# Matmul with batch norm: x and w loads on the SP and ACT queues, x casts on GpSimd, output copies on ScalarE

## The chip, the core and the metric

The kernel runs on one core of a Trainium2 chip. A core has five engines, each working through its own list of instructions in order: PE (TensorE, matmuls and transposes), DVE (VectorE), ACT (ScalarE), POOL (GpSimd) and SP (SyncE, which here only issues DMAs). Instructions on different engines wait for each other by semaphores; an instruction that waits holds up everything behind it on its engine. DMAs are issued from an engine's list and then run on 16 DMA engines that all queues share. The metric is the time of one execution in microseconds (us).

## The reference

```python
# x [16, 512, 1024], weight [1024, 768], gamma, beta [768], all f32
y = np.matmul(x, weight)                              # 8192 rows x 768 columns
mean = np.mean(y, axis=(0, 1), keepdims=True)         # one mean and variance per column
var = np.var(y, axis=(0, 1), keepdims=True)
y_norm = (y - mean) / np.sqrt(var + eps)
return (gamma * y_norm + beta).astype(np.float32)
```

No column can be normalized before its statistics over all 8192 rows are there.

## The kernel before

**Layout.** The 8192 rows of x are read in 32 loads of 256 rows (`load_x(q)`, L128, 1 MB each), two of which make one of 16 chunks of 512 rows (index c). The 768 columns are six tiles of 128 (index nt). The matmuls give y transposed, 128 columns by 512 rows, and one `mm(nt, c)` (L153) of eight matmuls is called a unit here. There are 96.

**A load.** A load is four DMAs, one for each quarter of k: quarter i goes into partitions 32i to 32i+31 of the tile `x_st`. Quarters 0 and 1 are issued by SP, 2 and 3 by POOL. The tile comes from the pool `stage`, which has three buffers; w loads (six, of 128 columns) and the output tiles `o_sb` use the same three. `cast_x(q, part)` (L133, ACT) turns half a load into bf16, `turn_x` (L147, DVE) turns it into `xT` by 32x32 blocks. `cast_w` (L120) is on DVE.

**A unit.** `mm` writes a PSUM tile `y_ps` (five buffers), `bn` (L159, DVE) takes its statistics, then `keep` (L164, ACT) copies it to SBUF as bf16 and frees it. In the program `keep` waits for `bn`.

**Two phases.** While x arrives, the first five chunks go through all six column tiles and the other eleven through tiles 0 to 2 (group A, 63 units in all). Then `finish` (L169 to L174) makes scale and shift for group A. Its output runs in 16 blocks of 512 rows beside the eleven units left of tile 3; then tile 3's output (eight blocks of 1024 rows) runs beside the units of tile 4, tile 4's beside those of tile 5, and tile 5's last. An output block is `norm` (L177, DVE), `turn_y` (L190, PE transposes into `o_ps`), `out_copy` (L198 on ACT or L200 on DVE, by turns) and `store` (L204, SP).

**Order.** Every step is put into a list of events with a due time worked out by hand (`at`, and the constants `W_US`, `Q_US`, `MM_US`). The list is sorted, and `seq` holds each engine to that order. So the numbers in the plan decide who stands behind whom in an engine's list, whatever the true durations are. `load_affine` (L103, L104) is one event with 12 small DMAs of gamma and beta on POOL, due when the last load has been planned.

Of the kernel before, what the change touches and what calls it, by code (L numbers as in the profile page):

```python
# [10 lines left out]
def kernel(  # L11
# [18 lines left out]
    nc = tc.nc  # L30
    f32 = mybir.dt.float32
# [8 lines left out]
    P = 128  # L40
    NT = N // P
    KQ = K // 4
    KT = K // P
# [4 lines left out]
    QU = QT // 2  # L48
    UP = 2
    QPC = CH // QR  # L50
    EARLY = 5
    STAGE = 3
    GA = 3
# [5 lines left out]
    stage = ctx.enter_context(tc.tile_pool(name="stage", bufs=STAGE))  # L59
    xbpool = ctx.enter_context(tc.tile_pool(name="xbpool", bufs=2))  # L60
    xtpool = ctx.enter_context(tc.tile_pool(name="xtpool", bufs=C - EARLY))
    ypool = ctx.enter_context(tc.tile_pool(name="ypool", bufs=(GA * C + (NT - GA) * EARLY) + 6))
    ypsum = ctx.enter_context(tc.tile_pool(name="ypsum", bufs=5, space=bass.MemoryType.PSUM))
# [21 lines left out]
    w_sb = singles.tile([P, KT, N], bf16)  # L85
# [10 lines left out]
    seq(nc.scalar.activation(warm, eps_sb, AF.Sqrt))  # L96


    xs, xb, xT, py, y, ops, ost, wst = {}, {}, {}, {}, {}, {}, {}, {}

    def load_affine():
# [3 lines left out]

    def load_w(part):

        n0 = part * P
        w_st = stage.tile([P, KT, P], f32, tag="st")
        wst[part] = w_st  # L110
        for i in range(4):
            eng = nc.sync if i < 2 else nc.gpsimd
            seq(eng.dma_start(  # L113
                w_st[32 * i:32 * i + 32],
                weight[KQ * i:KQ * (i + 1), n0:n0 + P].rearrange("(jj c) n -> c jj n", c=32),
            ))

    def cast_w(part):
        n0 = part * P
        seq(nc.vector.tensor_copy(w_sb[:, :, n0:n0 + P], wst.pop(part)))  # L120

    def load_x(q):
        x_st = stage.tile([P, QT, KQ], f32, tag="st")
        xs[q] = x_st
        rows = x_flat[q * QR:(q + 1) * QR].rearrange("(t r) k -> r t k", r=32)
        for i in range(4):
            eng = nc.sync if i < 2 else nc.gpsimd
            seq(eng.dma_start(x_st[32 * i:32 * i + 32], rows[:, :, KQ * i:KQ * (i + 1)]))  # L128

    def cast_x(q, part):  # L130
        x_bf = xbpool.tile([P, UP, KQ, 2], bf16, tag="xb")
        xb[q, part] = x_bf
        seq(nc.scalar.copy(  # L133
            x_bf.rearrange("p u k h -> p h u k"),
            xs[q].rearrange("p (h u) k -> p h u k", h=2)[:, :, part * UP:(part + 1) * UP, :],
        ))

    def turn_x(q, part):
        c, half = divmod(q, QPC)
        if half == 0 and part == 0:  # L140
            xT_sb = xtpool.tile([P, KT, CH], bf16, tag="xT")
            xT[c] = xT_sb
        src = xb.pop((q, part)).rearrange("p u k h -> p (u k h)").bitcast(f32)
        src = src.rearrange("p (u jj c) -> p u jj c", u=UP, c=32)
        dst = xT[c].rearrange("p jj m -> p (jj m)").bitcast(f32)
        dst = dst.rearrange("p (jj q u r) -> p q u jj r", jj=KT, q=QPC, r=32)
        seq(nc.vector.transpose(dst[:, half, part * UP:(part + 1) * UP], src))  # L147
# [64 lines left out]
    def at(t, fn, *args):  # L212
        events.append((t, len(events), fn, args))

    W_US, Q_US, MM_US = 1.0, 2.7, 1.75
    t = 0.0
    arrive = {}
    order = [("w", 0), ("w", 1), ("w", 2), ("x", 0), ("x", 1), ("w", 3), ("w", 4), ("w", 5)]
    order += [("x", q) for q in range(2, C * QPC)]
    freed = []  # L220
    for j, (kind, n) in enumerate(order):
        issue = t - 3.0
        if j >= STAGE:
            issue = max(issue, freed[j - STAGE] + 0.01)
        if kind == "w":
            at(issue, load_w, n)
            t += W_US
            at(t + 2.2, cast_w, n)
            freed.append(t + 2.2)
        else:  # L230
            at(issue, load_x, n)
            t += Q_US
            for part in range(QU // UP):
                at(t + 2.5 + 1.1 * part, cast_x, n, part)
                at(t + 3.7 + 1.1 * part, turn_x, n, part)
                freed.append(t + 2.5 + 1.1 * part) if part == QU // UP - 1 else None
            arrive[n] = t + 6.0

    at(t, load_affine)
    pe = 0.0  # L240
# [1 line left out]
    def unit(nt, c, span):  # L242
        nonlocal pe
        pe = max(pe, arrive[c * QPC + QPC - 1])
        at(pe, mm, nt, c)
        at(pe + 1.9, bn, nt, c)
        at(pe + 2.7, keep, nt, c)
        pe += span

    count = [0]  # L250

    def outputs(nts, t0, step, tiles, parts):

        rows = tiles * parts * P
        for b in range(M // rows):
            m0 = b * rows
            tb = t0 + step * b
            for c in range(m0 // CH, (m0 + rows) // CH):
                for nt in nts:
                    at(tb - 1.2, norm, nt, c)  # L260
            key = (nts[0], b)
            for part in range(parts):
                ti = tb + step / parts * part
                at(ti, turn_y, (key, part), nts, m0 + part * tiles * P, tiles)
                eng = "act" if count[0] % 2 == 0 else "dve"
                count[0] += 1
                at(ti + 0.9, out_copy, key, part, parts, eng)
            at(tb + step + 1.2, store, key, nts, m0, tiles * parts)

    for c in range(C):  # L270
        for nt in range(NT if c < EARLY else GA):
            unit(nt, c, MM_US)
    ga = list(range(GA))
    at(pe + 1.9, finish, ga)
    outputs(ga, pe + 6.0, 2.24, 2, 2)
    for nt in range(GA, NT):
        for c in range(EARLY, C):
# [42 lines left out]
```

## Time and profile before

| | |
|---|---|
| median of 3 runs | 311.28 us (309.02 to 312.35) |
| the profiled execution | 311.01 us |
| its span (first to last instruction) | 309.2 us |
| mean granted TensorE clock | 0.932 |
| PE busy, share of the span | 211.1 us, 68% |
| DVE busy | 172.5 us, 56% |
| ACT busy | 157.2 us, 51% |
| POOL busy | 51.6 us, 17% |
| HBM read, written | 36.71 MB, 25.17 MB |

The profiled execution lies 1.81 us above its own span (start and end), and 0.27 us below the median. Rows of a timeline give start, duration, engine, source line, operation, out<-in, shapes, count, and in brackets the idle time before with what ended it. Rows of the waits give who waited for whom, the sum in us, how often, and the longest. Rows of the groups give line, engine, operation, shapes and count, then busy us, mean ns of one, and idle us before with its releaser.

### The profile page before, as it was taken

What the parts mean: (1) busy time and instruction counts of PE and PEld (TensorE: products, weight loads), DVE (VectorE), ACT (ScalarE), POOL (GpSimd) and SP (SyncE); (2) the same over time, 40 slices, a digit from 0 to 9 for tenths busy, and PEclk for the clock granted to TensorE, in tenths of its full rate; (3) what the DMA queues carried; (4) which work ended last, traced back from release to release, by engine and by line L of the source; (5) the groups of instructions that cost most, each with busy time, mean ns of one, the idle gap of its engine ahead of it and who ended that gap; (6) DMA issues with size and microseconds to landing.
All of it is one profiled execution on the core that took longest, in us unless ns stands there. A gap on an engine that the chain in (4) does not pass through costs nothing.

```text
span 309.2 us, 3408 instructions
## 1 busy us (share of the span) xinstructions
PE 211.1 (68%) x1132; PEld 102.6 (33%) x1152; DVE 172.5 (56%) x312; ACT 157.2 (51%) x194; POOL 51.6 (17%) x95
## 2 busy tenths in 40 slices
PE   0006984667465658566855899998988999996630
PEld 0002432223222223222322344455544544543620
DVE  0131454535545455354454653689999866876851
ACT  1050667566766767657676753254553443434320
POOL 5414321212122122231225400000000000000000
PEclk9999999959999797998799999999999999998575
DMA  7999999999999999999999000029997884665698
GB/s 179 213 218 209 224 211 231 210 217 218 214 230 215 219 223 214 218 210 221 223 219 215 11 0 2 0 93 342 334 339 270 293 235 136 170 199 167 192 274 225
DMA packets 60177, 62.10 MB, mean 201 GB/s; under 512 B 3456, under 2 KB 55680, under 8 KB 60160
## 3 DMA queue, kind: packets, MB, share of 16 engines
q1 hardware_dynamic: 54080, 43.52, 57.2%
q0 software_dynamic: 6080, 18.36, 27.3%
q8 instruction: 9, 0.15, 0.2%
q14 instruction: 8, 0.07, 0.1%
HBM read 36.71 MB, written 25.17 MB: 200 GB/s over the span
## 4 chain that ended last, share of the span: by engine, by line
DMA 45%; PE 25%; ACT 11%; DVE 11%; issue 4%; POOL 1%; SPq 1%; ACTq 0%; DVEq 0%; POOLq 0%
DMA x_st<-in_x_dram 37%; PE y_ps L153 19%; ACT x_bf L133 9%; PE o_ps L190 6%; DMA w_st<-in_weight_dram 4%; DVE y_sb L177 4%; DVE o_sb L200 3%; DMA out_dram<-o_sb 3%; DVE stats L159 2%; ACT y_sb L164 1%; ACT o_sb L198 1%; SPq L128 1%; DVE mv L169 1%; POOL w_st L113 1%; DMA gamma_sb<-in_gamma_dram 1%
## 5 line engine op out<-in xcount | busy, mean ns | idle before, releaser
L153 PE MATMUL y_ps<-xT_sb,w_sb 128*128 128x512 bf16 x748 | 184.1, 397 | 73.9 <-ACT y_sb L164 45.7
L153 PEld LDWEIGHTS <-w_sb 128*128 128x128 bf16 x768 | 76.6, 101 | 169.8 <-issue 87.5
L133 ACT CAST x_bf<-x_st 128x1024 bf16<-128x1024 f32 x64 | 83.5, 1329 | 69.4 <-DMA x_st<-in_x_dram 66.1
L147 DVE STREAM_TRANSPOSE xT_sb<-x_bf 128x512 f32<-128x512 f32 x64 | 45.3, 709 | 79.5 <-ACT x_bf L133 79.5
L164 ACT CAST y_sb<-y_ps 128x512 bf16<-128x512 f32 x96 | 55.7, 580 | 49.6 <-DVE stats L159 49.6
L159 DVE BATCH_NORM_STATS2 stats<-y_ps 128x6 f32<-128x512 f32 x96 | 64.5, 676 | 15.5 <-PE y_ps L153 15.5
L128 POOL DMA_DIRECT2D x_st<-in_x_dram x64 | 37.1, 585 | 111.1 <-ACT x_bf L133 96.1
L190 PE MATMUL o_ps<-ident,y_sb 128*128 128x128 bf16 x384 | 34.5, 237 | 14.5 <-DVE y_sb L177 13.1
L200 DVE CAST o_sb<-o_ps 128x768 f32<-128x768 bf16 (+1 forms) x28 | 29.8, 1065 | 14.1 <-PE o_ps L190 5.9
L190 PEld LDWEIGHTS <-y_sb 128*128 128x128 bf16 x384 | 27.1, 106 | 26.8 <-DVE y_sb L177 21.0
L198 ACT CAST o_sb<-o_ps 128x768 f32<-128x768 bf16 (+1 forms) x28 | 25.0, 891 | 20.8 <-PE o_ps L190 11.9
L177 DVE TENSOR_SCALAR y_sb<-y_sb,scale,shift 128x512 bf16<-128x512 bf16 x96 | 33.6, 402 | 0.0
L120 DVE CAST w_sb<-w_st 128x1024 bf16<-128x1024 f32 x6 | 4.2, 694 | 20.6 <-DMA w_st<-in_weight_dram 20.6
L113 POOL DMA_DIRECT2D w_st<-in_weight_dram x12 | 7.3, 612 | 6.1 <-ACT x_bf L133 5.6
L103 POOL DMA_DIRECT2D gamma_sb<-in_gamma_dram x6 | 3.3, 551 | 3.4 <-DMA x_st<-in_x_dram 3.3
L104 POOL DMA_DIRECT2D beta_sb<-in_beta_dram x6 | 3.3, 547 | 1.9 <-DMA x_st<-in_x_dram 1.9
L170 ACT ACTIVATE std<-mv,eps_sb 128x1 f32<-128x1 f32 (+1 forms) x4 | 1.2, 295 | 4.1 <-DVE mv L169 4.1
L169 DVE BATCH_NORM_AGGREGATE mv<-stats 128x2 f32<-128x96 f32 x6 | 3.2, 561 | 0.0
L96 ACT ACT_TABLE_LOAD x1 | 1.3, 1283 | 0.7 <-PEq L301 0.7
L171 DVE RECIPROCAL scale<-std 128x1 f32<-128x1 f32 (+1 forms) x4 | 0.7, 166 | 1.4 <-ACT std L170 1.4
L173 DVE TENSOR_TENSOR tmp<-mv,scale 128x1 f32<-128x1 f32 (+1 forms) x4 | 0.6, 160 | 0.1
L174 DVE TENSOR_TENSOR shift<-beta_sb,tmp 128x1 f32<-128x1 f32 (+1 forms) x4 | 0.6, 160 | 0.1
(9 smaller groups left out, 1.8 us busy)
## 6 DMA issues: line engine op xcount, KB each, us to landing
x_st<-in_x_dram SPq DMA_DIRECT2D x64, 256.0 KB, 10.5
x_st<-in_x_dram POOLq DMA_DIRECT2D x64, 256.0 KB, 9.2
out_dram<-o_sb SPq DMA_DIRECT2D x16, 768.0 KB, 3.9
out_dram<-o_sb SPq DMA_DIRECT2D x24, 512.0 KB, 3.7
w_st<-in_weight_dram SPq DMA_DIRECT2D x12, 128.0 KB, 5.3
w_st<-in_weight_dram POOLq DMA_DIRECT2D x12, 128.0 KB, 5.7
gamma_sb<-in_gamma_dram POOLq DMA_DIRECT2D x6, 0.5 KB, 4.9
beta_sb<-in_beta_dram POOLq DMA_DIRECT2D x6, 0.5 KB, 4.2
```

The lines of the kernel that those rows point to most:

```text
L113: seq(eng.dma_start(w_st[32 * i:32 * i + 32], weight[KQ * i:KQ * (i + 1), n0:n0 + P].rearrange("(jj c) n -> c jj n", c=32),))
L128: seq(eng.dma_start(x_st[32 * i:32 * i + 32], rows[:, :, KQ * i:KQ * (i + 1)]))
L133: seq(nc.scalar.copy(x_bf.rearrange("p u k h -> p h u k"), xs[q].rearrange("p (h u) k -> p h u k", h=2)[:, :, part * UP:(part + 1) * UP, :],))
L147: seq(nc.vector.transpose(dst[:, half, part * UP:(part + 1) * UP], src))
L153: seq(nc.tensor.matmul(y_ps, w_sb[:, jj, nt * P:(nt + 1) * P], xT[c][:, jj, :], start=(jj == 0), stop=(jj == KT - 1),))
L159: seq(nc.vector.bn_stats(stats[:, nt, c, :], py[nt, c]))
L164: seq(nc.scalar.copy(y_sb, py.pop((nt, c))))
L169: seq(nc.vector.bn_aggr(mv[:, nt, :], stats[:, nt, :, :]))
L177: seq(nc.vector.tensor_scalar(y[nt, c], y[nt, c], scale[:, nt:nt + 1], shift[:, nt:nt + 1], op0=ALU.mult, op1=ALU.add,))
L190: seq(nc.tensor.transpose(o_ps[:, s, a, :], cols, ident))
L198: seq(nc.scalar.copy(ost[key][:, part], src))
L200: seq(nc.vector.tensor_copy(ost[key][:, part], src))
```

## The change

- Quarters 2 and 3 of every x and w load are issued by ACT, not POOL.
- w is loaded in three parts of 256 columns, not six of 128, into the pool of `xT` (11 buffers), not into `stage`. The order of loads is w0, x0, x1, w1, w2, x2 and so on (before: w0, w1, w2, x0, x1, w3, w4, w5).
- All `cast_x` are on POOL (`CAST` names the same copy twice).
- `out_copy` is on ACT for group A and tiles 3 and 4. For tile 5 it still alternates.
- The plan: `W_US` 2.7 for a part twice the size (was 1.0), `Q_US` 2.8 (was 2.7), start at 1.0, an x load due 0.2 after the planned start of the cast two loads before it.

```diff
-        w_st = stage.tile([P, KT, P], f32, tag="st")
+        w_st = xtpool.tile([P, KT, WN], f32, tag="xT")
...
-            eng = nc.sync if i < 2 else nc.gpsimd
+            eng = nc.sync if i < 2 else nc.scalar
...
+    CAST = [nc.gpsimd.tensor_copy, nc.gpsimd.tensor_copy]
...
-        seq(nc.scalar.copy(
+        copy = CAST[part]
+        seq(copy(
...
-    W_US, Q_US, MM_US = 1.0, 2.7, 1.75
-    t = 0.0
+    W_US, Q_US, MM_US = 2.7, 2.8, 1.75
+    t = 1.0
...
+            at(begun[-2] + 0.2 if len(begun) >= 2 else t - 4.0, load_x, n)
             t += Q_US
+            begun.append(t + 2.5)
             for part in range(QU // UP):
-                at(t + 2.5 + 1.1 * part, cast_x, n, part)
-                at(t + 3.7 + 1.1 * part, turn_x, n, part)
+                at(t + 2.5 + 1.2 * part, cast_x, n, part)
+                at(t + 3.8 + 1.2 * part, turn_x, n, part)
...
-                eng = "act" if count[0] % 2 == 0 else "dve"
+                eng = "act" if nts[0] < NT - 1 or count[0] % 2 == 0 else "dve"
```

New line numbers: `load_x` L130, `cast_x` L136, `turn_x` L150, `bn` L162, `keep` L167, `finish` L172 to L177, `norm` L180, `out_copy` L201 and L203, `load_affine` L105 and L106.

First place: POOL's list at the end of the loads. The four casts below are the two halves of load 30 (`x_st_971`) and of load 31 (`x_st_1007`, the last). Before, POOL ended so:

```order
L128 DMA x_st_947<-in_x_dram 32x8x256 x2
L128 DMA x_st_981<-in_x_dram 32x8x256 x2
L103 DMA gamma_sb_86<-in_gamma_dram 128x1
L104 DMA beta_sb_87<-in_beta_dram 128x1
...
```

Now it ends so; "..." stands for five more pairs of the gamma and beta rows:

```order
L136 CAST x_bf_1022<-x_st_946 128x2x512
L136 CAST x_bf_1037<-x_st_971 128x2x512
L105 DMA gamma_sb_86<-in_gamma_dram 128x1
L106 DMA beta_sb_87<-in_beta_dram 128x1
...
L136 CAST x_bf_1054<-x_st_971 128x2x512
L136 CAST x_bf_1071<-x_st_1007 128x2x512
L136 CAST x_bf_1083<-x_st_1007 128x2x512
```

The 12 small DMAs stood behind everything POOL had to do; now three of the 64 casts stand behind them.

Second place: DVE's list at the same point, where the last four `turn_x` stand among the `bn`. Before:

```order
L147 STREAM_TRANSPOSE xT_sb_1048<-x_bf_1020 128x2x8x32
L147 STREAM_TRANSPOSE xT_sb_1048<-x_bf_1046 128x2x8x32
L159 BN_STATS stats_84<-y_ps_1036 128x6
L147 STREAM_TRANSPOSE xT_sb_1048<-x_bf_1062 128x2x8x32
L159 BN_STATS stats_84<-y_ps_1053 128x6
L147 STREAM_TRANSPOSE xT_sb_1048<-x_bf_1067 128x2x8x32
L159 BN_STATS stats_84<-y_ps_1070 128x6
```

Now:

```order
L150 STREAM_TRANSPOSE xT_sb_1056<-x_bf_1037 128x2x8x32
L162 BN_STATS stats_84<-y_ps_1028 128x6
L150 STREAM_TRANSPOSE xT_sb_1056<-x_bf_1054 128x2x8x32
L162 BN_STATS stats_84<-y_ps_1058 128x6
L150 STREAM_TRANSPOSE xT_sb_1056<-x_bf_1071 128x2x8x32
L162 BN_STATS stats_84<-y_ps_1073 128x6
L150 STREAM_TRANSPOSE xT_sb_1056<-x_bf_1083 128x2x8x32
L162 BN_STATS stats_84<-y_ps_1088 128x6
```

Of group A's 63 `bn`, 47 stood ahead of the last `turn_x` and 16 behind it; now it is 50 and 13. Ahead of the last but two (the one that reads `x_bf_1054`, the first behind POOL's small DMAs) stand 48.

Third place: ACT's list where group A's output begins. Before, every second output copy was here and the other on DVE:

```order
L164 CAST y_sb_1299<-y_ps_1286 128x512
L198 CAST o_sb_1317<-o_ps_1301 128x768
L164 CAST y_sb_1338<-y_ps_1308 128x512
L198 CAST o_sb_1340<-o_ps_1331 128x768
L198 CAST o_sb_1371<-o_ps_1363 128x768
```

Now both copies of a block are here:

```order
L167 CAST y_sb_1281<-y_ps_1268 128x512
L201 CAST o_sb_1299<-o_ps_1283 128x768
L201 CAST o_sb_1299<-o_ps_1304 128x768
L167 CAST y_sb_1320<-y_ps_1290 128x512
L201 CAST o_sb_1322<-o_ps_1313 128x768
L201 CAST o_sb_1322<-o_ps_1336 128x768
```

In the load phase ACT's list held two casts per x load among the `keep`; now it holds two DMA issues per x load in their stead.

More of the change, by code (lines that the diff above doesn't have):

```diff
@@ L50 @@
     QPC = CH // QR
+    WN = 256
     EARLY = 5
@@ L106, in load_w @@
     def load_w(part):
-        n0 = part * P
-        w_st = stage.tile([P, KT, P], f32, tag="st")
+        n0 = part * WN
+        w_st = xtpool.tile([P, KT, WN], f32, tag="xT")
         wst[part] = w_st
         for i in range(4):
-            eng = nc.sync if i < 2 else nc.gpsimd
+            eng = nc.sync if i < 2 else nc.scalar
             seq(eng.dma_start(
                 w_st[32 * i:32 * i + 32],
-                weight[KQ * i:KQ * (i + 1), n0:n0 + P].rearrange("(jj c) n -> c jj n", c=32),
+                weight[KQ * i:KQ * (i + 1), n0:n0 + WN].rearrange("(jj c) n -> c jj n", c=32),
             ))
     def cast_w(part):
-        n0 = part * P
-        seq(nc.vector.tensor_copy(w_sb[:, :, n0:n0 + P], wst.pop(part)))
+        n0 = part * WN
+        seq(nc.vector.tensor_copy(w_sb[:, :, n0:n0 + WN], wst.pop(part)))
     def load_x(q):
@@ L126, in load_x @@
         for i in range(4):
-            eng = nc.sync if i < 2 else nc.gpsimd
+            eng = nc.sync if i < 2 else nc.scalar
             seq(eng.dma_start(x_st[32 * i:32 * i + 32], rows[:, :, KQ * i:KQ * (i + 1)]))
@@ L213, in at @@
         events.append((t, len(events), fn, args))
-    W_US, Q_US, MM_US = 1.0, 2.7, 1.75
-    t = 0.0
+    W_US, Q_US, MM_US = 2.7, 2.8, 1.75
+    t = 1.0
     arrive = {}
-    order = [("w", 0), ("w", 1), ("w", 2), ("x", 0), ("x", 1), ("w", 3), ("w", 4), ("w", 5)]
+    order = [("w", 0), ("x", 0), ("x", 1), ("w", 1), ("w", 2)]
     order += [("x", q) for q in range(2, C * QPC)]
[L220 to L224, printed above, removed]
+    begun = []
+    for kind, n in order:
         if kind == "w":
-            at(issue, load_w, n)
+            at(t - 4.0, load_w, n)
             t += W_US
             at(t + 2.2, cast_w, n)
-            freed.append(t + 2.2)
         else:
-            at(issue, load_x, n)
+            at(begun[-2] + 0.2 if len(begun) >= 2 else t - 4.0, load_x, n)
             t += Q_US
+            begun.append(t + 2.5)
             for part in range(QU // UP):
-                at(t + 2.5 + 1.1 * part, cast_x, n, part)
-                at(t + 3.7 + 1.1 * part, turn_x, n, part)
-                freed.append(t + 2.5 + 1.1 * part) if part == QU // UP - 1 else None
-            arrive[n] = t + 6.0
+                at(t + 2.5 + 1.2 * part, cast_x, n, part)
+                at(t + 3.8 + 1.2 * part, turn_x, n, part)
+            arrive[n] = t + 6.2
     at(t, load_affine)
```

## Prediction

> **What bounds the kernel now.** I read the page's forty slices first (7.73 us each), because a mean over the span hides its stages.
>
> ```profile
> PE   0006984667465658566855899998988999996630
> DMA  7999999999999999999999000029997884665698
> GB/s 179 213 218 209 224 211 231 210 217 218 214 230 215 219 223 214 218 210 221 223 219 215 11 0 2 0 93 342 334 339 270 293 235 136 170 199 167 192 274 225
> ```
>
> Three stages stand out: 22 slices (170 us) with full DMA engines at about 218 GB/s and PE half idle; four without DMA and PE full; then stores beside a nearly full PE. The windows view gives these stages numbers (busy us and instructions by engine, PE clock, DMA share, GB/s).
>
> ```profile
> 60.00:120.00 60.00, 37.84 (x142) 15.32 (x144) 28.11 (x44) 39.09 (x44) 14.76 (x26) 0.89 1.09 218
> ...
> 172.00:198.00 26.00, 24.46 (x112) 11.12 (x114) 13.01 (x21) 12.36 (x20) 2.68 (x5) 1.00 0.01 1
> 198.00:234.00 36.00, 32.68 (x255) 18.90 (x259) 34.14 (x74) 16.92 (x26) 0.00 (x0) 1.00 0.71 257
> 234.00:260.00 26.00, 23.20 (x158) 12.23 (x159) 19.88 (x42) 11.48 (x18) 0.00 (x0) 1.00 0.73 232
> 260.00:285.00 25.00, 21.92 (x147) 11.73 (x150) 18.54 (x39) 10.65 (x17) 0.00 (x0) 0.99 0.61 175
> ```
>
> ```profile
> HBM read 36.71 MB, written 25.17 MB: 200 GB/s over the span
> ```
>
> While x loads, the DMAs are the bound: 36.7 MB at 218 GB/s are 168 us, and no engine is busy for more than two thirds (ACT 39.1 of 60). From 198 to 234 DVE is busy 34.1 of 36 us, PE 32.7. From 234 to 285 PE is (45.1 of 51).
>
> What the end of the loads hands on is seen in the timeline (first number: start). The ACT rows are first halves of loads 29, 30 and 31; the DVE rows the last `turn_x`, the `bn` behind it, the last `bn` of group A, and its aggregate.
>
> ```profile
> 163.24 1.33 ACT L133 CAST x_bf<-x_st 128x1024 bf16<-128x1024 f32 x1 [1.27 <-DMA x_st<-in_x_dram]
> ...
> 167.86 1.32 ACT L133 CAST x_bf<-x_st 128x1024 bf16<-128x1024 f32 x1 [1.61 <-DMA x_st<-in_x_dram]
> ...
> 172.69 1.33 ACT L133 CAST x_bf<-x_st 128x1024 bf16<-128x1024 f32 x1 [1.38 <-DMA gamma_sb<-in_gamma_dram]
> ...
> 174.51 25.84 PE L153 MATMUL y_ps<-xT_sb,w_sb 128*128 128x512 bf16 x117 [1.43 <-ACT y_sb L164]
> ...
> 175.73 0.71 DVE L147 STREAM_TRANSPOSE xT_sb<-x_bf 128x512 f32<-128x512 f32 x1 [0.38 <-ACT x_bf L133]
> 176.37 3.05 DVE L159 BATCH_NORM_STATS2 stats<-y_ps 128x6 f32<-128x512 f32 x5
> ...
> 195.43 0.70 DVE L159 BATCH_NORM_STATS2 stats<-y_ps 128x6 f32<-128x512 f32 x1 [1.03 <-PE y_ps L153]
> ...
> 197.16 0.70 DVE L159 BATCH_NORM_STATS2 stats<-y_ps 128x6 f32<-128x512 f32 x1 [1.03 <-PE y_ps L153]
> 197.77 1.47 DVE L169 BATCH_NORM_AGGREGATE mv<-stats 128x2 f32<-128x96 f32 x3
> ```
>
> A load arrives every 4.7 us. A unit costs 1.73 us (195.43 to 197.16). PE runs unbroken from 174.51, and the last unit of group A is its thirteenth: 174.51 + 13 x 1.73 = 197.0. Why ten units more than the last chunk's three are left by then, the waits of the whole span tell (who waited for whom, sum, times, longest):
>
> ```profile
> DVE xT_sb L147 <- ACT x_bf L133: 79.5, 56, 5.6
> ACT x_bf L133 <- DMA x_st<-in_x_dram: 66.1, 30, 12.8
> ACT y_sb L164 <- DVE stats L159: 49.6, 42, 2.8
> PE y_ps L153 <- ACT y_sb L164: 45.7, 25, 4.1
> ```
>
> Read from below: PE waits for `keep`, `keep` for `bn`, and `bn` stands in DVE's list behind a `turn_x` that waits for a cast, which waits for a load. So PE runs at most five units (the PSUM buffers) ahead of the place that the plan gave `bn`, and this backlog at the end of the loads sets when group A is done.
>
> **The change, part by part**, against the profiled execution's 311.0 us (span 309.2), 0.3 below the median.
>
> *The queues.* The two that now carry the loads (q1 is SP's, q0 POOL's; packets, MB, share of the 16 engines, 60 to 120 us):
>
> ```profile
> q1 hardware_dynamic: 6890, 6.64, 59.5%
> q0 software_dynamic: 1952, 6.42, 49.4%
> ```
>
> q1 takes 0.595 x 960 / 6.64 = 86 engine-us per MB, q0 74. ACT's queue is hardware like SP's, and no row shows two of these beside each other. Bounds: if all loads cost q1's price at the same summed share of 1.09, the rate is 16 x 1.09 / 86 = 203 GB/s and the loads end 12.6 us later; at q0's price it is 236, 12.8 us earlier. I take 218, the row of two queues at work together: 0. The issues themselves, priced like POOL's,
>
> ```profile
> L128 POOL DMA_DIRECT2D x_st<-in_x_dram x64 | 37.1, 585 | 111.1 <-ACT x_bf L133 96.1 <-DVE w_sb L120 10.4 <-issue 4.7
> ```
>
> put 64 x and 6 w issues, 41 us, on ACT, which loses 83.5 us of casts: room is there. New is that an issue on ACT waits for a tile of `stage`, that is for the cast three loads back, with `keep` queued behind it and PE behind `keep`. But that `keep` waits anyway for a `bn` behind a `turn_x` of about that load. The other way round, an issue stuck behind a `keep` leaves a load in flight (4.7 us of bytes) to cover it. I put both at 0; without this cover each microsecond would show in the loads. The new order of w0, x0, x1 and the three larger `cast_w` move PE's first units, but the DMAs are full from the second slice on either way: 0.
>
> *The casts.* The groups show the ACT cast, `keep`, a DVE cast of the same size, and on POOL the small DMAs, the select, a wide memset and a narrow one (mean ns behind the comma).
>
> ```profile
> L133 ACT CAST x_bf<-x_st 128x1024 bf16<-128x1024 f32 x64 | 83.5, 1329 | 69.4 <-DMA x_st<-in_x_dram 66.1 <-issue 2.0 <-DMA gamma_sb<-in_gamma_dram 1.4
> ...
> L164 ACT CAST y_sb<-y_ps 128x512 bf16<-128x512 f32 x96 | 55.7, 580 | 49.6 <-DVE stats L159 49.6
> ...
> L120 DVE CAST w_sb<-w_st 128x1024 bf16<-128x1024 f32 x6 | 4.2, 694 | 20.6 <-DMA w_st<-in_weight_dram 20.6
> L103 POOL DMA_DIRECT2D gamma_sb<-in_gamma_dram x6 | 3.3, 551 | 3.4 <-DMA x_st<-in_x_dram 3.3
> L104 POOL DMA_DIRECT2D beta_sb<-in_beta_dram x6 | 3.3, 547 | 1.9 <-DMA x_st<-in_x_dram 1.9
> ...
> masks.py:199 POOL TENSOR_SCALAR_AFFINE_SELECT ident<-ident 128x128 bf16<-128x128 bf16 x1 | 0.3, 304 | 0.1
> ...
> masks.py:197 POOL MEMSET ident<- 128x128 bf16 x1 | 0.2, 204 | 0.3 <-POOLq L301 0.3
> ...
> L84 POOL MEMSET eps_sb<- 128x1 f32 x1 | 0.1, 99 | 0.0
> ```
>
> From the two memsets an element costs (204 - 99) / 127 = 0.83 ns, so 1024 take 0.95 us: the lower end. The select scaled by eight gives 2.43 us: the upper. I take 1.4, by the same cast on ACT. Two casts are 2.8 us of each 4.7: covered by the DMAs, and the cover ends at 2.35 us a cast. The Trainium skill speaks against this move: GPSIMD Engine Reference, section Key points, has DVE about twice as fast elementwise. By that, an estimate: 2 x 0.694 = 1.39 us a cast, still under the loads; no run here shows it.
>
> *POOL's small DMAs.* Twelve at 0.55 us are 6.6 us. Before, they stood behind everything. Now they stand behind the first cast of load 30 and ahead of the last three casts. That cast starts at 167.9 and ends at 169.3; the DMAs end at 175.9; the next cast ends at 177.3, its `turn_x` (0.71) at 178.0. Until then DVE's list is stuck with 48 `bn` done, and PE fills its five buffers and stops. Then one `bn` (0.70) and one `keep` (0.58) free a buffer at 179.3. PE has units 54 to 63 left, ten: 179.3 + 17.3 = 196.6, against 197.0. The better order (13 `bn` behind the last `turn_x`, not 16) is thus eaten by the small DMAs: **-0.4 us**. The cast's time enters twice: this part is -1.3 at 0.95 us and +1.7 at 2.43.
>
> *The output copies.* From 198 to 234 DVE loses its copies and ACT gets them. The groups of the two copies of 128x768, and DVE's copies in this window alone (busy us, count):
>
> ```profile
> L200 DVE CAST o_sb<-o_ps 128x768 f32<-128x768 bf16 x16 | 15.2, 948 | 1.6 <-PE o_ps L190 1.1 <-issue 0.5
> ...
> L198 ACT CAST o_sb<-o_ps 128x768 f32<-128x768 bf16 x16 | 12.8, 800 | 8.1 <-PE o_ps L190 6.5 <-DMA out_dram<-o_sb 1.6
> ...
> 198.00:234.00 36.00, 12.32 (x13) 1.00 0.71 257
> ```
>
> DVE falls from 34.1 to 21.8 us of 36, ACT rises by 13 x 0.80 to 27.3. Next in line is PE (32.7) and the stores (slices at 334 to 342 GB/s). What can be won is PE's idle time that DVE ends, from 198 to 285:
>
> ```profile
> PE o_ps L190 <- DVE y_sb L177: 7.5, 10, 2.3
> ```
>
> That is the upper end, 7.5 us: `norm` stands behind a copy that itself waits for PE. The lower end is a loss: both copies of a block now stand ahead of a `keep` on ACT, and if PE waited 0.8 us for each of tile 3's eleven, it would be +8.8; five PSUM buffers speak against it. I take a third of the gain, **-2.5 us**, as PE and stores are close behind. The tail (tile 5, from 285) keeps its alternation: 0.
>
> Sum: 311.0 - 0.4 - 2.5 = **308.1 us**.
>
> **Rivals.** *Dearer loads (slower).* Both halves in hardware queues: if the price goes to q1's 86, the loads end 12.6 us later, POOL's late casts and PE's last ten units move along, and the time is 320.7. For it: q1 has a higher price in every row. Against: part of this is the other queue's packets in between. It decides from 211 GB/s on down (36.7 / 211 is 174 us, 6 more than 168, which outweighs the gain and 1%). I put its middle at 317.
>
> *Faster loads.* The same engines move 342 GB/s in the store slices, so 218 isn't their limit. If the two queues' packets overlap better when they are alike, up to q0's price, it's 308.1 - 12.8 = 295.3; the middle, 300. The Trainium skill bears on this: SBUF — State Buffer, section "Can I just issue two DMAs to hit both halves?", says that a second DMA to the other half of the partitions adds 6%, so a queue for each half would bring little. By it, an estimate: 231 GB/s and 9.4 us less, if the 218 doesn't hold it already; the trace, with two queues on two halves since before, can't tell.
>
> *A slow cast.* Over 2.35 us POOL is the bound of the loads: at 2.8 it adds 64 x 0.45 = 29 us to the 308.1, plus twice 1.4 at the small DMAs: 340. The select's row alone points there.
>
> *Nothing gained at the output.* If ACT's order costs what DVE's relief brings, it's 310.6; with a loss of 3, 314.
>
> **How the numbers follow.** A measurement of this kernel tells about 1% from no change: 308.2 to 314.4 is the same. Forecast 44% (305 to 311), dearer loads 20% (312 to 321), faster loads 13% (295 to 303), slow cast 8% (over 321), nothing at the output 15% (309 to 315). Half of the forecast's 44 and all 13 are faster: 35%. The other half, 12 of the output's 15 and 5 of the dearer loads' 20 are the same: 39%. The remaining 15 and 3 and the slow cast's 8 are slower: 26%. The range leaves out the slow cast and the lower half of the faster loads: 299 to 321.
>
> **What would show it.** GB/s from 60 to 120 us: 218, or 203 to 211 for the dear loads, over 225 for the fast ones. POOL's cast near 1.4 us. A hole of 6.6 us in POOL's casts after the first half of load 30, and PE idle in it; the aggregate of group A at 197. PE's wait for `norm` near 5 us from 198 to 285, DVE near 22 of 36 us in the first output window. I am wrong if ACT's DMA issues wait for a `keep` longer than a load lasts and the DMA share falls under 1.0, or if the first aggregate moves by more than 3 us at an unchanged rate.

## The result and the profile after

| | before | after |
|---|---|---|
| median | 310.6 us (4 runs, 309.02 to 312.35) | 296.15 us (4 runs, 291.19 to 297.9) |
| ratio | | 0.943, 95% interval 0.930 to 0.957 |
| profiled execution, span | 311.01, 309.2 us | 297.9, 296.1 us |
| last x packet lands (read from the packets of the trace) | 171.6 us | 163.6 us |
| first aggregate (group A) starts | 197.77 us | 193.18 us |
| first to fourth aggregate | 86.96 us | 78.92 us |
| fourth aggregate to the end of the span | 24.5 us | 24.0 us |

By the medians the change is faster by 14.5 us, where 2.9 were forecast (311.0 to 308.1); 296.15 lies below the range of 299 to 321. The ratios leave out executions over 1.5% above the fastest of their kernel (of the change 297.48 us and the profiled 297.9, so that its ratio stands for 17.6 us and its profile for 13.1; of e12 too the profiled 300.95), and of the profiles of e4 (750.6 us) and e14 (381.7 us), where a unit's matmul took 1104 and 582 ns on average (before: 397), only the loads of e14 are read.

Of the 13.1 us by which the span is shorter, 4.6 are there at the first aggregate, 8.0 come between it and the fourth, 0.5 behind.

**The loads.** The slices of the page after (7.40 us each) and its windows:

```profile
GB/s 175 304 232 297 208 251 264 220 209 211 206 203 213 235 220 225 231 220 221 223 231 170 3 1 2 0 0 265 360 357 363 259 278 217 178 197 179 281 265 215
```

```profile
10.00:30.00 20.00, 9.06 (x29) 3.55 (x29) 7.34 (x10) 1.26 (x3) 7.68 (x6) 1.00 1.12 279
...
60.00:120.00 60.00, 43.09 (x171) 17.71 (x174) 29.01 (x46) 11.59 (x21) 32.42 (x26) 0.91 1.12 215
```

Slices of 304 and 297 GB/s stand among the first, and later all is as before: 215 from 60 to 120 us, where before had 218. The DMA share is 1.12 in both windows, so on average the engines are not short of work; the same packets take less time in the first window. The loads end 8.0 us earlier: SP's last packet lands at 159.9, but ACT's at 163.6. This is won within the first 60 us, at 244 GB/s where before had 212.

**The end of the loads**, in the timeline after (load 29, load 30's first half, first and last of POOL's small DMAs, the last three casts, PE, the aggregate):

```profile
154.51 2.55 POOL L136 CAST x_bf<-x_st 128x1024 bf16<-128x1024 f32 x2 [2.23 <-DMA x_st<-in_x_dram]
...
162.29 1.33 POOL L136 CAST x_bf<-x_st 128x1024 bf16<-128x1024 f32 x1 [5.22 <-DMA x_st<-in_x_dram]
...
163.53 0.68 POOL L105 DMA_DIRECT2D gamma_sb<-in_gamma_dram  x1
...
169.47 0.53 POOL L106 DMA_DIRECT2D beta_sb<-in_beta_dram  x1
170.00 3.80 POOL L136 CAST x_bf<-x_st 128x1024 bf16<-128x1024 f32 x3
...
173.33 2.29 PE L156 MATMUL y_ps<-xT_sb,w_sb 128*128 128x512 bf16 x5 [5.82 <-ACT y_sb L167]
...
193.18 1.46 DVE L172 BATCH_NORM_AGGREGATE mv<-stats 128x2 f32<-128x96 f32 x3
```

The first half of load 30 is cast at 162.29, 5.6 us earlier than before (167.86), though the loads end 8.0 earlier: load 30 comes late. By the DMAs' semaphores in the trace it is complete at 162.1, and load 31 only 2.1 us later, at 164.2 (before: 167.8 and 172.6). POOL's small DMAs then hold the last three casts until 170.0, and PE waits until 173.3.

Why load 30 is so late is seen in the issues (ACTq and SPq rows) after:

```profile
138.51 15.87 SPq L130 DMA_DIRECT2D x_st<-in_x_dram  x8
...
148.21 8.04 ACTq L130 DMA_DIRECT2D x_st<-in_x_dram  x2
156.41 0.34 ACTq L130 DMA_DIRECT2D x_st<-in_x_dram  x1
158.16 0.32 ACTq L130 DMA_DIRECT2D x_st<-in_x_dram  x1
```

and in the waits after:

```profile
ACT y_sb L167 <- DMA x_st<-in_x_dram: 92.6, 20, 23.2
...
PE y_ps L156 <- ACT y_sb L167: 43.3, 22, 7.7
```

SP has issued all by 154.4; ACT's quarters of load 31 go at 156.4 and 158.2. The row of 148.21 covers ACT's two issues of load 30 and the wait between them, 8 us, where an issue takes 0.3. The second of them waits on a semaphore that in this program SP's first quarter of the same load uses too; that one lands at 155.9, and ACT's issue follows at 155.93. `keep` waits behind such issues, 92.6 us in all, though PE's own wait for `keep` is no longer than before (43.3 us, 45.7 before).

**The output.** Windows from the first to the fourth aggregate of before and of after, then PE's waits after in it:

```profile
197.77:284.73 86.96, 77.76 (x557) 42.68 (x566) 72.53 (x153) 39.10 (x60) 0.00 (x0) 1.00 0.69 225
```

```profile
193.18:272.10 78.92, 74.42 (x559) 42.80 (x567) 51.77 (x130) 55.22 (x82) 0.00 (x0) 1.00 0.76 247
```

```profile
PE o_ps L193 <- DVE y_sb L180: 2.7, 3, 1.3
PE o_ps L193 <- ACT o_sb L201: 0.9, 2, 0.7
```

DVE falls by 20.8 us, ACT rises by 16.1, and PE's idle time falls from 9.2 to 4.5 (its wait for `norm` from 7.5 to 2.7). PE's busy time falls too, by 3.3 us.

### The profile page after: what moved, and what is told of

Same layout as the page of the kernel before. It is cut to its first block, busy times and chain, and to the rows that moved or that the text cites. A ratio compares the mean times of both kernels' runs of the same rounds, so it can differ in the third digit from the quotient of the medians.

```text
span 296.1 us, 3319 instructions
## 1 busy us (share of the span) xinstructions
PE 210.9 (71%) x1132; PEld 102.7 (35%) x1152; DVE 149.6 (51%) x285; ACT 99.4 (34%) x154; POOL 89.3 (30%) x83
## 3 DMA queue, kind: packets, MB, share of 16 engines
q1 hardware_dynamic: 52448, 43.52, 57.3%
## 4 chain that ended last, share of the span: by engine, by line
DMA 56%; PE 26%; DVE 6%; POOL 5%; ACT 4%; issue 2%; ACTq 0%; SPq 0%; DVEq 0%; POOLq 0%
DMA x_st<-in_x_dram 46%; PE y_ps L156 23%; DMA out_dram<-o_sb 8%; PE o_ps L193 3%; ACT o_sb L201 3%; POOL x_bf L136 3%; DMA w_st<-in_weight_dram 2%; DVE y_sb L180 2%; DVE stats L162 1%; POOL beta_sb L106 1%; POOL gamma_sb L105 1%; DVE o_sb L203 1%; ACT y_sb L167 1%; DVE mv L172 0%; DVE xT_sb L150 0%
## 5 line engine op out<-in xcount | busy, mean ns | idle before, releaser
L156 PE MATMUL y_ps<-xT_sb,w_sb 128*128 128x512 bf16 x748 | 187.9, 403 | 65.5 <-ACT y_sb L167 43.3
L156 PEld LDWEIGHTS <-w_sb 128*128 128x128 bf16 x768 | 77.6, 103 | 164.2 <-issue 82.5
L167 ACT CAST y_sb<-y_ps 128x512 bf16<-128x512 f32 x96 | 56.0, 588 | 163.4 <-DMA x_st<-in_x_dram 92.6
L136 POOL CAST x_bf<-x_st 128x1024 bf16<-128x1024 f32 x64 | 82.1, 1328 | 84.0 <-DMA x_st<-in_x_dram 81.8
L150 DVE STREAM_TRANSPOSE xT_sb<-x_bf 128x512 f32<-128x512 f32 x64 | 45.4, 711 | 82.0 <-POOL x_bf L136 82.0
L162 DVE BATCH_NORM_STATS2 stats<-y_ps 128x6 f32<-128x512 f32 x96 | 65.0, 678 | 36.5 <-PE y_ps L156 36.2
L201 ACT CAST o_sb<-o_ps 128x768 f32<-128x768 bf16 (+1 forms) x52 | 44.9, 886 | 24.5 <-DMA out_dram<-o_sb 13.0
L193 PE MATMUL o_ps<-ident,y_sb 128*128 128x128 bf16 x384 | 31.2, 231 | 9.8 <-DVE y_sb L180 6.9
L180 DVE TENSOR_SCALAR y_sb<-y_sb,scale,shift 128x512 bf16<-128x512 bf16 x96 | 33.2, 404 | 0.0
L193 PEld LDWEIGHTS <-y_sb 128*128 128x128 bf16 x384 | 26.2, 104 | 19.1 <-DVE y_sb L180 9.3
L122 DVE CAST w_sb<-w_st 128x2048 bf16<-128x2048 f32 x3 | 3.7, 1228 | 12.1 <-DMA w_st<-in_weight_dram 12.1
L203 DVE CAST o_sb<-o_ps 128x1024 f32<-128x1024 bf16 x4 | 4.9, 1225 | 6.1 <-DMA out_dram<-o_sb 5.2
L105 POOL DMA_DIRECT2D gamma_sb<-in_gamma_dram x6 | 3.4, 559 | 0.0
L106 POOL DMA_DIRECT2D beta_sb<-in_beta_dram x6 | 3.2, 536 | 0.0
L172 DVE BATCH_NORM_AGGREGATE mv<-stats 128x2 f32<-128x96 f32 x6 | 3.2, 561 | 0.0
L177 DVE TENSOR_TENSOR shift<-beta_sb,tmp 128x1 f32<-128x1 f32 (+1 forms) x4 | 0.6, 160 | 0.1
L175 DVE TENSOR_TENSOR scale<-scale,gamma_sb 128x1 f32<-128x1 f32 (+1 forms) x4 | 0.6, 159 | 0.1
```

The source lines that it names most:

```text
L105: seq(nc.gpsimd.dma_start(gamma_sb[:, nt:nt + 1], gamma[nt * P:(nt + 1) * P, None]))
L106: seq(nc.gpsimd.dma_start(beta_sb[:, nt:nt + 1], beta[nt * P:(nt + 1) * P, None]))
L122: seq(nc.vector.tensor_copy(w_sb[:, :, n0:n0 + WN], wst.pop(part)))
L136: seq(copy(x_bf.rearrange("p u k h -> p h u k"), xs[q].rearrange("p (h u) k -> p h u k", h=2)[:, :, part * UP:(part + 1) * UP, :],))
L156: seq(nc.tensor.matmul(y_ps, w_sb[:, jj, nt * P:(nt + 1) * P], xT[c][:, jj, :], start=(jj == 0), stop=(jj == KT - 1),))
L162: seq(nc.vector.bn_stats(stats[:, nt, c, :], py[nt, c]))
```

## The experiments

The runs came in four groups, each beside fresh runs of before on its chip (medians 310.8 to 312.7 us), so the ratio is what compares them. GB/s is that of 60 to 120 us; the landing of the last x packet, on whichever queue, and the first aggregate are those of the profiled execution (for e4 and e5 that of e5, the ratio that of e4).

| run | median us | ratio (95%) | GB/s | x landed | aggregate |
|---|---|---|---|---|---|
| the change | 296.15 | 0.943 (0.930 to 0.957) | 215 | 163.6 | 193.2 |
| e1 loads on POOL's queue | 306.6 | 0.968 (0.960 to 0.976) | 223 | 168.0 | 196.0 |
| e2 copies split | 302.3 | 0.967 (0.960 to 0.973) | 220 | 159.6 | 190.3 |
| e3 before, copies | 303.6 | 0.971 (0.962 to 0.979) | 217 | 172.3 | 198.8 |
| e4, e5 before, queues | 295.1, 294.4 | 0.945 (0.939 to 0.950) | 251 | 155.5 | 181.8 |
| e6 before, both | 286.4 | 0.920 (0.914 to 0.926) | 250 | 154.9 | 181.5 |
| e7 casts on ACT | 301.4 | 0.971 (0.962 to 0.979) | 204 | 173.5 | 195.7 |
| e8 small DMAs early | 288.4 | 0.927 (0.919 to 0.935) | 223 | 160.9 | 183.2 |
| e9 e7, issue behind the cast | 283.3 | 0.915 (0.909 to 0.920) | 244 | 156.4 | 180.4 |
| e10 e6, SP alone | 311.3 | none (301.4 to 314.7 us) | 209 | 180.4 | 206.8 |
| e11 e6, quarters swapped | 312.9 | 1.013 (1.007 to 1.019) | 205 | 182.1 | 208.3 |
| e12 e6, casts on POOL | 296.7 | 0.955 (0.949 to 0.961) | 225 | 165.5 | 195.2 |
| e13 e6, columns swapped | 287.5 | 0.924 (0.914 to 0.933) | 248 | 156.3 | 182.7 |
| e14 e6, blocks swapped | 312.6 | 1.007 (1.003 to 1.012) | 206 | 179.7 | (disturbed) |
| e15 e3, quarters swapped | 300.8 | 0.968 (0.959 to 0.976) | 223 | 168.0 | 194.3 |

### Each half undone, and each half alone: e1 to e4

e1, in `load_w` and `load_x`:

```diff
-            eng = nc.sync if i < 2 else nc.scalar
+            eng = nc.sync if i < 2 else nc.gpsimd
```

> The change with its second quarters of every load back on POOL's queue (POOL then issues them and casts). Theory 'two hardware queues': the gain of the load phase comes from the pair SP and ACT, so here the rate falls back to about 218 GB/s between 60 and 120 us, the last load ends near 170 us instead of 160, the first aggregate near 198 to 200 instead of 193, and the time is 5 to 8 us above the change's. Rival 'order and casts': the gain of the loads comes from the new order of the w and x loads and from ACT freed of casts; then the rate stays above 225 and the time within 2 us of the change's.

The ratio is 2.5 hundredths above the change's, about 7.7 us (3.2 between the two profiled executions), and the loads end 4.4 us later; e2, whose lists are those of the change until the first aggregate, has them at 159.6, 8.4 earlier than here, so a few microseconds between two profiles are spread. The second hardware queue thus brings the larger part of the loads' gain; what is left in e1 (168.0 against 171.6 before) would be that of the new order and the thirds. The rate I named tells nothing: 223 here, 215 in the change. The loss is in the first 60 us, 218 GB/s here against 244, and it is seen best from 10 to 30 us, where the change has 279 and before 216:

```profile
10.00:30.00 20.00, 1.97 (x5) 0.81 (x6) 5.01 (x6) 0.00 (x0) 8.59 (x9) 1.00 1.08 243
```

e2, in `outputs`:

```diff
-                eng = "act" if nts[0] < NT - 1 or count[0] % 2 == 0 else "dve"
+                eng = "act" if count[0] % 2 == 0 else "dve"
```

> The change with the output copies alternating between ACT and DVE as before. Theory 'copies': about 8 us of the gain come from DVE's relief between 193 and 275 us, so the time is 6 to 9 us above the change's, with the first aggregate still at 193 and the stretch from the first aggregate to the second back from 30 to about 35 us. Rival 'a free ACT': the output stage gained because ACT has no casts and fewer leftovers then; the time is within 2 us of the change's.

2.3 hundredths, 7.3 us, and the window between the aggregates is that of before to 0.01 us:

```profile
190.30:277.27 86.97, 77.76 (x558) 42.64 (x567) 72.53 (x152) 39.10 (x60) 0.00 (x0) 1.00 0.69 225
```

e3 is the same line the other way round, in the kernel before:

```diff
-                eng = "act" if count[0] % 2 == 0 else "dve"
+                eng = "act" if nts[0] < NT - 1 or count[0] % 2 == 0 else "dve"
```

> The kernel before with only the output copies of all tiles but the last moved to ACT. Theory 'copies': 6 to 9 us faster than before (302 to 305), with the first aggregate unmoved at 197 to 198 and the stretch from it to the second shortened from 36 to about 30 us. My prediction's own term was 2.5 us (308). Rival: the gain needs the other parts too, under 2 us.

8.2 us below before, and the window as in the change:

```profile
198.84:278.18 79.34, 74.37 (x559) 42.80 (x567) 51.78 (x130) 55.22 (x82) 0.00 (x0) 1.00 0.75 245
```

With the same copies the stretch takes 87.0 us in both kernels, with the others 79.3 and 78.9. The copies' share is 8 us, and the rest of the change doesn't move it; "a free ACT" falls.

e4, the kernel before:

```diff
-            eng = nc.sync if i < 2 else nc.gpsimd
+            eng = nc.sync if i < 2 else nc.scalar
```

> The kernel before with only the loads' second quarters moved from POOL's queue to ACT's (ACT still casts). Theory 'two hardware queues': the rate rises where both queues are active at once, at least in the first 60 us (above 235 GB/s), and the loads end 5 to 12 us earlier than at 171.6. But ACT's list, with casts and keeps ahead of its issues, may put the queues out of step, which would hold the gain down; then the rate is above 230 in the first 60 us and about 215 later. Rival 'order and casts': the rate stays at 218 all through.

295.1 us: this one word, in `load_w` and `load_x`, is worth 16.8 us, as much as the whole change (ratios 0.945 and 0.943). My fear that casts and keeps ahead of ACT's issues put the queues out of step did not come true here.

### What the rest of the change costs: e5 to e8

e5 is e4 once more, for its profile.

> The kernel before with only the loads' second quarters on ACT's queue once more, for a profile at the usual clock. Theory 'two hardware queues': near 295 us; rate from 60 to 120 us above 235 GB/s and the loads' end more than 12 us before 171.6. Rival 'output freed': the loads end within 5 us of 171.6 and the gain lies behind the first aggregate.

```profile
GB/s 175 195 217 207 210 253 258 243 258 252 260 233 257 266 238 235 259 247 246 247 260 14 0 2 0 0 321 336 341 336 232 302 180 176 158 208 146 206 281 233
```

```profile
60.00:120.00 60.00, 43.89 (x170) 17.97 (x172) 32.76 (x51) 45.80 (x50) 0.00 (x0) 0.91 1.01 251
```

251 GB/s held to the end, at a DMA share of 1.01 (before: 218 at 1.09). The loads end 16.1 us earlier, and the first aggregate comes 16.0 earlier.

e6 is e3's and e4's edits together.

> The kernel before with both: the loads' second quarters on ACT's queue, and the output copies of all tiles but the last on ACT; casts on ACT, w in sixths and the order of the loads as before. If the two gains add (16.8 and 8.2 us off 311.9), 287, and what the change has beyond the two (casts on POOL, w in thirds, the other order) costs it some 9 us. If the two gains overlap, 294 to 297, and the rest of the change costs nothing.

286.4 us: the gains add (287 expected). The change, with the same two edits, is 2.3 hundredths (7 us) above it, so its other parts cost that much.

e7, the change with:

```diff
-    CAST = [nc.gpsimd.tensor_copy, nc.gpsimd.tensor_copy]
+    CAST = [nc.scalar.copy, nc.scalar.copy]
```

> The change with the x casts on ACT instead of POOL, nothing else. POOL then issues its small DMAs without a cast behind them. Theory 'POOL's casts cost': the time falls to 287 to 291. Rival 'ACT's list': with casts as well, ACT's issues come later, the queues get further out of step, and the time rises above 298. If neither: within 2 us of the change's 296, and what costs the change its gain is the order of the loads or the w thirds.

The rival holds: 301.4 us, and the lowest rate yet.

```profile
60.00:120.00 60.00, 39.77 (x147) 15.94 (x148) 26.77 (x43) 37.90 (x43) 0.00 (x0) 0.86 1.14 204
```

What that rate is made of is seen in the DMA view of two microseconds, 106 to 108 (packets, MB, share of the 16 engines; q1 is SP's queue, q10 ACT's):

```profile
q1 hardware_dynamic: 378, 0.37, 100.3%
q10 hardware_dynamic: 53, 0.05, 13.6%
```

The queues take turns: here SP's has seven eighths of the bytes, from 104 to 105 ACT's has nine tenths. Counted from the packets in half microseconds from 60 to 120 us, the lesser queue has over a quarter of the bytes in 21% of them; in e6 it is 54%. ACT issues its first quarter of a load 2.1 us (median) behind SP's here, 0.0 in e6.

e8, the change with:

```diff
-    at(t, load_affine)
+    at(-10.0, load_affine)
```

> The change with POOL's twelve small DMAs issued at the start of the program instead of between the casts of load 30; nothing else moves in any engine's list. Theory 'hole': the 6.6 us between cast(30,0) and the next cast vanish; the last casts follow load 31 (landed by 160), the first aggregate comes about 5 us earlier (188 instead of 193), and the time falls to 290 to 292. Rival 'backlog': PE's units left at the end of the loads set the aggregate whatever the last casts do; within 2 us of the change's time.

```profile
159.61 5.07 POOL L136 CAST x_bf<-x_st 128x1024 bf16<-128x1024 f32 x4 [5.08 <-DMA x_st<-in_x_dram]
```

```profile
183.21 1.46 DVE L172 BATCH_NORM_AGGREGATE mv<-stats 128x2 f32<-128x96 f32 x3
```

The four casts run without a hole. From load 30's first cast to the aggregate are 23.6 us (the change: 30.9), and the time falls to 288.4, some 5 us by the ratios (1.6 hundredths; the intervals overlap from 0.930 to 0.935). That is most of the 7 us that the change loses to e6. It is more than I expected (188 for the aggregate, 290 to 292 us); part of it are loads that ended 2.7 us earlier, which is within the spread between two profiles.

### In step, and which half: e9 to e12

e9 is e7 with the place of the loads in the plan moved:

```diff
-            at(begun[-2] + 0.2 if len(begun) >= 2 else t - 4.0, load_x, n)
+            at(begun[-3] + 1.21 if len(begun) >= 3 else t - 4.0, load_x, n)
```

> The change with its x casts on ACT (the run before it, 301.4 us at 204 GB/s from 60 to 120 us) and, as the one new edit, each load's issues planned right behind the last cast of the load three back, not behind the first cast of the load two back. Theory 'in step': SP's and ACT's issues are then released by the same cast, both queues carry packets at the same time, the rate from 60 to 120 us returns to about 250 GB/s, the loads end near 150 to 155 us, and the time falls to 282 to 287. Rival 'thirds and order': the w thirds and the order of the loads put the queues out of step for good; the rate stays under 225 and the time above 297.

```profile
60.00:120.00 60.00, 43.02 (x183) 18.16 (x182) 32.67 (x51) 46.06 (x51) 0.00 (x0) 0.97 0.99 244
```

The same two microseconds, 106 to 108:

```profile
q1 hardware_dynamic: 271, 0.26, 62.0%
q10 hardware_dynamic: 227, 0.22, 49.8%
```

One line takes 17 us off e7 (5.6 hundredths) and makes the fastest of all these kernels, 283.3 us (the interval of e6's ratio overlaps). In e7 ACT issued its half of a load only behind the first cast of the load two back, that is when that load had landed, while SP was ahead; now one cast releases both, and ACT's first issue of a load comes 0.0 us behind SP's. The lesser queue has over a quarter of the bytes in 57% of the half microseconds. "In step" stands.

e10, in e6:

```diff
-            eng = nc.sync if i < 2 else nc.scalar
+            eng = nc.sync
```

> The kernel before with the output copies on ACT and all loads on SP's queue. Theory 'one queue at a time is worth 205': the rate from 60 to 120 us is 200 to 210 GB/s, as in the run with the queues in turns, and the time 8 to 14 us above the 303.6 of the copies alone (312 to 318). Rival 'the rate is that of the 16 engines': it stays at 218 or above, and the time within 2 us of 304.

```profile
60.00:120.00 60.00, 38.95 (x147) 15.31 (x145) 27.40 (x43) 38.56 (x42) 0.00 (x0) 0.89 1.14 209
```

One queue alone gives 209, about what two give in turns. The time, 311.3, is 7.7 us above e3's, just under the 8 to 14 that I expected.

e11, in e6:

```diff
-            eng = nc.sync if i < 2 else nc.scalar
+            eng = nc.sync if i % 2 == 0 else nc.scalar
```

> The kernel before with the output copies on ACT and two hardware queues (286.4 us), but SP takes quarters 0 and 2 of each load and ACT 1 and 3, so that each queue writes both halves of the partitions. Theory 'two queues at once': which quarters a queue has doesn't matter; rate 245 to 255 GB/s, time within 2 us of 286.4. Rival 'two halves': it is the two partition halves written at the same time that give the rate; with the same half written by both queues at a time the rate falls to 215 or below and the time rises to 300 or more.

Here my theory fell in the form it had. Two hardware queues, each with half of the bytes (packets, MB, share, 60 to 120 us):

```profile
q10 hardware_dynamic: 6388, 6.16, 57.8%
q1 hardware_dynamic: 6325, 6.09, 55.9%
```

and 205 GB/s, 312.9 us. SP now writes partitions 0 to 31 while ACT writes 32 to 63, then both go to the upper half. The queues are not out of step here: ACT's first issue comes 0.0 us behind SP's, and the lesser queue has over a quarter of the bytes in 81% of the half microseconds. So two queues at once are not enough; for the gain each has to keep to one half.

e12, in e6 (the second line so that nothing stands among the casts):

```diff
-        seq(nc.scalar.copy(
+        seq(nc.gpsimd.tensor_copy(
...
-    at(t, load_affine)
+    at(-10.0, load_affine)
```

> The kernel before with the output copies on ACT and two hardware queues (286.4 us), and now the x casts on POOL, with the twelve small DMAs at the start of the program so that they don't stand among the casts. Theory 'in step': without casts ACT's issues stand among keeps alone, which wait for other things than SP's issues do, the queues fall out of step, the rate from 60 to 120 us drops from 250 to 215 to 230 GB/s, and the time rises to 290 to 295. Rival 'casts are free anywhere': rate 245 or more, time within 2 us of 286.4; then the change's own order of issues is what costs it the rate.

```profile
60.00:120.00 60.00, 40.69 (x160) 16.80 (x159) 29.40 (x46) 11.03 (x20) 32.62 (x26) 0.83 1.11 225
```

```profile
158.86 0.59 ACT L164 CAST y_sb<-y_ps 128x512 bf16<-128x512 f32 x1 [10.05 <-DMA x_st<-in_x_dram]
```

The rate falls from 250 to 225 and the time rises by 3.5 hundredths, 11 us, more than the 4 to 9 that I expected: besides the rate, `keep` stands 10 us behind a DMA issue at the end of the loads. So the casts on POOL cost twice, neither time by their own length. From 60 to 120 us ACT's first issue of a load comes 0.0 to 5.7 us behind SP's, where in e6 it is 0.0 for every load: without a cast in ACT's list, nothing brings ACT's issues into line with SP's. That the missing cast is the reason, and not the semaphores that the two queues share, is argued and not tested by itself.

### Halves or columns: e13 to e15

In e11 the halves and the columns of x and w that a queue reads changed together. e13, in e6, for x and w alike:

```diff
+    SRC = [0, 2, 1, 3]
...
-            seq(eng.dma_start(x_st[32 * i:32 * i + 32], rows[:, :, KQ * i:KQ * (i + 1)]))
+            seq(eng.dma_start(x_st[32 * i:32 * i + 32], rows[:, :, KQ * SRC[i]:KQ * (SRC[i] + 1)]))
```

> The kernel before with the output copies on ACT and two hardware queues (286.4 us); SP still writes partitions 0 to 63 and ACT 64 to 127, but from other columns of x and w: blocks of 32 partitions get k quarters 0, 2, 1, 3 (for w too, so the sums are the same). Theory 'partition halves': 245 to 255 GB/s from 60 to 120 us and 286 +- 2 us. Rival 'columns': what counts is which columns of a row are read at the same time; as with the swapped quarters 205 GB/s and above 305 us.

```profile
60.00:120.00 60.00, 41.73 (x174) 17.52 (x176) 32.73 (x51) 46.61 (x50) 0.00 (x0) 0.97 1.09 248
```

e14 is e13 with e11's line, so that SP reads columns as in e6 but writes blocks 0 and 2.

> The complement: SP reads k quarters 0 and 1 and ACT 2 and 3 as in the 286.4 us kernel, but SP writes partition blocks 0 and 2, ACT 1 and 3. Theory 'partition halves': both queues write the lower half together and then the upper, so 200 to 210 GB/s and 308 to 315 us. Rival 'columns': 245 to 255 GB/s and 286 +- 2 us.

```profile
60.00:120.00 60.00, 57.43 (x149) 19.81 (x151) 27.16 (x42) 38.59 (x42) 0.00 (x0) 0.56 1.14 206
```

It is the partition blocks (four of 32 partitions, 0 to 3) that decide: 248 with the columns swapped, 206 with the blocks swapped (its timed runs give 312.6 us, as e11). Why is open. That two halves are written at one moment doesn't explain it alone: by a count of e11's packets (256 to each DMA of x), SP was in block 2 beside ACT in block 1, or in 0 beside 3, for 24 of the 120 half microseconds, two different halves, and these ran at 201 to 202 GB/s too. Other shares of the four blocks were not run.

e15, in e3:

```diff
-            eng = nc.sync if i < 2 else nc.gpsimd
+            eng = nc.sync if i % 2 == 0 else nc.gpsimd
```

> The kernel before with the output copies on ACT (303.6 us), loads on SP's and POOL's queues as before, but SP has quarters 0 and 2 and POOL 1 and 3. Theory 'halves count for any pair': the 218 GB/s of before hold a part of the same gain, which goes: 200 to 210 GB/s and 308 to 318 us. Rival 'POOL's queue gains nothing from the other half': 215 to 221 GB/s and within 2 us of 303.6.

```profile
60.00:120.00 60.00, 39.05 (x151) 15.98 (x154) 28.05 (x44) 41.04 (x46) 13.89 (x24) 0.91 1.09 223
```

223 GB/s and 300.8 us, nothing lost (e3: 217 and 303.6; the ratios' intervals overlap). The pair of before, SP's and POOL's queues, never had the gain of the two halves. It isn't out of step: POOL issues its half 0.3 us (median) behind SP's, in before and here.

## Why the prediction was wrong, step by step

Between the 308.1 us forecast and the 297.9 of the profiled execution lie 10.2 us. The output copies are 5.5 of them (-8.0 where -2.5 was taken), the way to the first aggregate 4.2 (-4.6 where -0.4 was taken), the tail 0.5. So two terms failed: the rate of the loads, put at 0, and the size of the copies' gain.

- **The rate of the loads (taken: 0): this step failed.** I carried 218 GB/s, the row of a hardware and a software queue, over to two hardware queues. Their rate is 204 to 251, by whether each keeps to one half and both run in step. My upper end, 236 at POOL's price per byte, was no bound either: in e6 the shares and MB of 60 to 120 us give 67 and 62 engine-us per MB, both under POOL's 74. In the change the loads end 8.0 us earlier, and load 30's first cast comes 5.6 earlier. "Faster loads", at 13%, has the measured time in its range, but by luck: 8.0 of the 13.1 us are the copies', and its sign, over 225 GB/s from 60 to 120 us, did not show. Of its mechanism, that packets of two alike queues overlap better, e11 shows that alike is not enough. Against "dearer loads" I could have read more: "a higher price in every row" holds for the rows of the loads, but over the whole span q1, stores included, takes 65 engine-us per MB (57.2% of 16 x 309.2 by 43.52 MB) and q0 74. The rows of e6, 60 to 120 us:

```profile
q1 hardware_dynamic: 7728, 7.44, 52.2%
q10 hardware_dynamic: 7835, 7.55, 48.4%
```

- **Its sign would have been missed.** I named the rate from 60 to 120 us, and it stayed at 215; the gain lay ahead of it. That it came out near the 218 taken is luck: a pair of queues that can do 250 ran out of step. The other condition that I named did show: the first aggregate moved by 4.6 us.
- **ACT's issues (taken: 0): right as delays, wrong as to what they do.** I looked at issues and keeps as delays, each covered by a load in flight, and PE's wait for `keep` did not grow (43.3 us, 45.7 before). What they cost is the step of the two queues: e9 against e7 is 17 us. This error and the one on the rate pull in opposite directions, and from 60 to 120 us they cancel.
- **POOL's cast (taken: 1.4): right.** 64 casts took 82.1 us:

```profile
L136 POOL CAST x_bf<-x_st 128x1024 bf16<-128x1024 f32 x64 | 82.1, 1328 | 84.0 <-DMA x_st<-in_x_dram 81.8
```

  The Trainium skill's GPSIMD Engine Reference, section Key points, agrees: 1.33 us are 1.9 times DVE's 0.694.
- **POOL's small DMAs (net -0.4): the hole was right, the net off by 1.4 us.** It is there as described, 163.5 to 170.0, and PE restarts 11.0 us behind load 30's first cast (11.4 forecast). From that cast to the aggregate are 30.9 us, 29.9 before: +1.0. What I didn't see is that this hole would eat what faster loads bring; e8 shows it by taking it out.
- **The output copies (taken: -2.5): mechanism right, size wrong; the largest miss of the sum.** 8.0 us, as e2 and e3 show each for itself. I took a third of 7.5 "as PE and stores are close behind". They were, but not in the way: stores rose to 363 GB/s, and PE was rid of 4.7 us of idle and 3.3 of busy time; my upper end counted idle time alone. Why transposes take less PE time (25.5 us before, 22.9 after in the windows) wasn't tested. The loss that I set against it, a `keep` behind copies, isn't among PE's waits of this window at all; PE waits 0.9 us for a copy. Of the signs that I named, PE's wait for `norm` is 2.7 us, not 5.
- **The tail (0): right**, 24.5 and 24.0.

Sum by the profiled executions: 311.0 - 5.6 (load 30's first cast) + 1.0 (from there to the aggregate) - 8.0 (output) - 0.5 (tail) = 297.9.

## What to carry to other kernels

Load from two hardware queues, one for each half of the partitions, and have both halves of a load released by the same instruction: 244 to 251 GB/s here, 204 to 225 when either condition fails. When engines change roles, look at what else stands in their lists: the small DMAs among POOL's casts cost some 5 us, and the casts that left ACT's list took with them what kept the queues in step. For an engine that hands work to the bound engine at every block, a third of the bound engine's wait was too little: here PE lost half of its idle time in the stretch (4.7 of 9.2 us) and 3.3 us of busy time that no term held.

## What the hardware showed that I had not expected

- Two hardware queues, each kept to one half of the partitions and issued in step, move 244 to 251 GB/s (e5, e6, e9, e13); when each writes into both halves 205 and 206 (e11, e14), in turns 204 (e7), SP alone 209 (e10). The Trainium skill says in SBUF — State Buffer, section "Can I just issue two DMAs to hit both halves?", that a second DMA at partition 64 brought only 6%, "they serialize"; the runs here show 20% (250 by 209), and the measurement decides. It also says in DMA: Bandwidth & Descriptors, section "Issuing engines are not separate DMA queues", that issuing from several engines saves only the time to issue; e4, which changes nothing but the issuing engine of half of the loads, is 16.8 us faster, by the rate of its loads (e5: 251 against 218).
- SP's hardware queue with POOL's software queue stays at 217 to 223 whichever partitions each writes (before, e3, e15). Why the software queue doesn't gain is open. It is issued in step; one difference in the rows is the packets, 3.3 KB each on POOL's queue and 1.0 KB on SP's (6.42 MB by 1952, 6.64 by 6890), whose effect wasn't tested.
- The DMA share does not show which case it is: from 60 to 120 us it reads 1.14 at 204 GB/s (e7) and 1.01 at 250 (e6), and 1.09 both at 218 (before) and at 248 (e13). So a share over 1 here does not say that the engines move all they can.
